# First weight sum of a Strassen piece by an adding DMA, mixer tiles that share homes, and one more k-tile pair per unit in that form

## The chip, the cores and the metric

One core of a Trainium2 chip runs the whole program. The metric is the time of one execution in device microseconds; a kernel's time is the median of its runs. Engines are named as in the profile: PE (matrix), DVE (vector), ACT (scalar), POOL (GpSimd), SP (which issues most loads).

## The reference

One layer of a decoder trunk in float32: batch 1, 256 positions (S), width 4096 (D), two token mixers of width 2048 side by side.

```
u    = rmsnorm(x) * norm_w
proj = u @ w_in                          # 4096 x 24576
a_q, a_f, a_i, a_g, b_q, b_k, b_v, b_g, gate_a, gate_b = split(proj)
o_a  = rmsnorm(hgrn2(a_q, a_f, a_i)) * silu(a_g)          # 16 heads of 128, chunks of 64
o_b  = rmsnorm(diff_attention(a pair of maps, ALiBi)) * 0.8 * silu(b_g)   # 8 heads of 2 x 128
y    = sigmoid(gate_a) * (o_a @ w_branch_a) + sigmoid(gate_b) * (o_b @ w_branch_b)
out  = rmsnorm(x + y @ w_out) * final_w
```

The four matrix products read some 537 MB of weights; everything between them is small.

## The kernel before

**Units and pieces.** The weights come as 512 *pieces*, each a pair of k-tiles (2 x 128 rows) by 1024 columns: a tile `w` of 128 x 2048 floats, one load of 1 MB. A *unit* makes 256 x 1024 outputs, in four PSUM banks of 128 x 512 (block 2t+n: row half t, column half n). There are 16 mixer units (`w_mix`; 16 pieces each), 8 gate units (`w_gate`; 16), 8 branch half units (`w_branch`; 8) and 4 output units (`w_out`; 16). `run` (L245) goes through the pieces in order.

**Three products for one.** Every float32 operand is split into hi (its value rounded to the multiplier's format) and lo (the rest), and each product is hi·hi + hi·lo + lo·hi: three matmuls (L289). Weights are split as they come: ACT writes `hi` (L165), DVE `lo` = w - hi (L166), in chunks of 1024 columns. In the mixers and in gate 0 `hi` and `lo` have five buffers each, from gate 1 on seven (L978).

**Two forms of a piece.** A plain piece (P) is two chunks and 2 x 4 blocks x 3 = 24 matmuls. A Strassen piece (S, Winograd's form with seven products in place of eight) is 7 x 3 = 21 matmuls, for which weights and activations are first added up. Its activation sums are made once per k-tile pair (`s_form`, L378, tile `sf`). Its weight sums are made for each piece (`sums`, L142, all on DVE): L146 adds two quarters of the tile in place, L147 subtracts a third from that into a tile `wt`, L151 subtracts `wt` from two quarters in place. Then four chunks are split, the third of 512 columns (`wt`), the others of 1024. PE takes the chunks in this order, and ORDER (L266) says into which banks: chunk 0 to p5 and P1 (two helper banks), chunk 1 to blocks 0 and 1, chunk 2 to P6, chunk 3 to P7 and block 2.

**Which pieces are S.** SPLIT = (4, 6, 8, 10, 12, 13) in mixer units 3 to 15 and in gates 0 and 1, SPLIT_G = (0, 2, 4, 6, 8, 10, 12, 13, 14) in gates 2 to 6, Y_SPLIT = (0, 2, 4, 6, 8, 10, 12) in output units 1 to 3: 13 x 6 + 12 + 45 + 21 = 156 pieces.

**Raw tiles and queues.** `w` has three buffers. SP issues the load of piece k as soon as the last `lo` of piece k-3 has been made (L133), so each buffer goes round: load, split, load. POOL issues the writes to DRAM (`g_dram` L374, `o_dram` L708, `h_dram` L612) and a few masks (L828, L894) in program order; a POOL instruction that waits holds up all behind it. Evictions and splits are recorded at a higher priority (L158, L293), and the order on each engine follows from that.

**End of a unit.** The last piece is held back and run block by block, (0,0), (0,1), (1,0), (1,1), six matmuls each, so that banks are emptied while PE goes on. In a unit with S pieces P6 and P7 go through DVE (L318 to L324) as soon as the last S piece is done, then the four blocks (L372 in a gate, then the sigmoid on ACT, L373, and the write, L374). Which block of the next unit PE starts with follows from the order in which the banks are emptied.

**Mixers.** Eight groups of two units: four HGRN2, four attention. Between the matmuls of a unit `step` (L224) hands out small jobs from a list. Each group's tiles come from `tmp`, one buffer for each tag; `finish` (L673) makes the norm, the gate and the transposed output.

Of the kernel before, what the change touches and what calls it, by code (L numbers as in the profile page):

```python
# [37 lines left out]
SPLIT_AHEAD = 3  # L38
# [5 lines left out]
def trunk_kernel(ctx, tc, xT, x, nw, w_mix, w_gate, w_branch, w_out, lbt, hnw, lamv, slw, fw, out):  # L44
# [8 lines left out]
    wt = ctx.enter_context(tc.tile_pool(name="wt", bufs=1))  # L53
    sp = ctx.enter_context(tc.tile_pool(name="sp", bufs=6))
# [41 lines left out]
    class Stream:  # L96
# [3 lines left out]

        def __init__(self):
# [19 lines left out]
        def load_to(self, n):  # L121
            while self.loaded < min(n, len(self.src)):
# [4 lines left out]
                if i > 1:  # L127
                    m = HALF if i < HEAD else PIECE
                    for c in range(0, PIECE, m):
                        self.load_part(i, c, m)  # L130
# [11 lines left out]
        def sums(self, i, c):  # L142
            w = self.raw[i]
            if c == 0:
                t = self.raw[i, "T"] = wt.tile([P, 512], F32, name="wt", tag="wt")
                dve.tensor_tensor(w[:, 0:512], w[:, 0:512], w[:, 512:1024], op=ALU.add)  # L146
                dve.tensor_tensor(t, w[:, 0:512], w[:, 1536:2048], op=ALU.subtract)  # L147
            if c == 2:
                t = self.raw[i, "T"]
                b = w[:, 512:1536].rearrange("p (a c) -> p a c", a=2)  # L150
                dve.tensor_tensor(b, b, t.unsqueeze(1).to_broadcast([P, 2, 512]), op=ALU.subtract)  # L151

        def split_to(self, n):
            while self.done < min(n, len(self.chunks)):
# [3 lines left out]
                with tc.high_priority(AHEAD):  # L158
                    if self.kind[i] == "S":
                        self.sums(i, c)  # L160
                    t = self.raw[i, "T"] if c == 2 else self.raw[i][:, (0, 1024, 0, 512)[c] :]
# [5 lines left out]
                if c == (3 if self.kind[i] == "S" else 1):  # L167
                    del self.raw[i]
                    self.raw.pop((i, "T"), None)
# [96 lines left out]
    ORDER = (("p5", "P1"), (0, 1), ("P6",), ("P7", 2))  # L266
# [174 lines left out]
    SPLIT = (4, 6, 8, 10, 12, 13)  # L441
    SPLIT_G = (0, 2, 4, 6, 8, 10, 12, 13, 14)
    us = {}
    s_pools = [sp] * 6
# [19 lines left out]
    def more_sums(n):  # L464
        if n == 0:
            s_pools[:] = [sp2] * 3
# [50 lines left out]
    def branch_unit(q):  # L517
# [28 lines left out]
        def post(n):  # L546
            if n == 0:
                g_load(0)
                if q == 0:
                    o_end()  # L550
                    s_pools[:] = [sp] * 6 + [sp2]
# [106 lines left out]
    with tc.tile_pool(name="tmp", bufs=1) as tmp:  # L658
# [8 lines left out]
        def half(tag):  # L667
            return tmp.tile([P, HPG, P], F32, name=tag, tag=tag)

# [3 lines left out]
        def finish(T, seg, eps, scale, slot):  # L673

            n = 1024 // seg
            o, sq, g = T["o"], T["sq"], T["g"]

            def stats():
                ss = tmp.tile([P, n], F32, name="ss", tag="ss", bufs=2)
                dve.tensor_reduce(ss, fl(sq).rearrange("p (n c) -> p n c", c=seg), axis=AX.X, op=ALU.add)  # L680
                act.activation(ss, ss, AF.Sqrt, scale=1.0 / seg, bias=eps)
                dve.reciprocal(ss, ss)
                T["ss"] = ss

            def gate():
                sg = big("z")
# [344 lines left out]
```

## Time and profile before

| | |
|---|---|
| median of 3 runs | 2794.47 us (2794.36 to 2796.64) |
| the profiled execution's own time | 2795.3 us |
| its span in the trace | 2793.6 us |
| PE, DVE, ACT, POOL busy | 99%, 79%, 57%, 3% |
| granted PE clock | 0.999 |
| bytes moved | 597.76 MB, mean 214 GB/s |

The span leaves 1.7 us of the execution's time outside. Matmuls overlap in the trace, so PE's rate is read from the time of a long row of them, and its waits from gaps that the trace lists. In the stretch from 278.5 to 1587.6 us the mixer units with S pieces and gates 0 and 1 run; gates 2 to 6 from 1587.6 to 2003 us; the branches from 2091 to 2445 us; the output units to the end.

### The profile page before, as it was taken

To read this page: it belongs to the slowest core of one execution; us is meant where nothing else is said; L and a number is where in the kernel's file an instruction comes from. 1 tells how busy PE (TensorE), PEld (TensorE's weight loads), DVE (VectorE), ACT (ScalarE), POOL (GpSimd) and SP (SyncE) were. 2 spreads that over 40 slices of the span, in tenths; PEclk is the share of its full clock that TensorE was granted. 3 is DMA by queue.
4 is the path that set the end of the run, shared out by engine and by line. 5 is a ranking of instruction groups with operands and counts; after the bars stand their busy time and mean duration, and the time that the engine had idled before them with its cause. 6 is when DMAs were issued, how large, how long until landed. Compare 5 with 4: busy or idle time off the path is not lost.

```text
span 2793.6 us, 32659 instructions
## 1 busy us (share of the span) xinstructions
PE 2770.9 (99%) x12418; PEld 2285.5 (82%) x12418; DVE 2219.3 (79%) x2502; ACT 1578.5 (57%) x1877; POOL 75.0 (3%) x124
## 2 busy tenths in 40 slices
PE   9999999999999999999999999999999999999998
PEld 7888888888888888888888888778888888888886
DVE  6784888888888888888888999999855555668997
ACT  7664656556556555565556555555553444445554
POOL 0010000000000000000000000000000000010000
PEclk9999999999999999999999999999999999999999
DMA  9555555554555555555456555555676666665665
GB/s 351 190 179 192 181 195 189 211 203 181 196 189 208 198 177 203 194 198 201 181 192 239 224 199 208 226 219 203 253 260 220 230 223 234 240 244 212 249 250 217
DMA packets 96767, 597.76 MB, mean 214 GB/s; under 512 B 11857, under 2 KB 12129, under 8 KB 31201
## 3 DMA queue, kind: packets, MB, share of 16 engines
q1 hardware_dynamic: 88272, 566.29, 56.3%
q0 software_dynamic: 8336, 29.38, 2.8%
q8 instruction: 97, 1.59, 0.2%
q14 instruction: 62, 0.50, 0.1%
HBM read 571.51 MB, written 24.12 MB: 213 GB/s over the span
## 4 chain that ended last, share of the span: by engine, by line
PE 84%; DVE 10%; DMA 3%; issue 1%; ACT 1%; POOL 0%; DVEq 0%; ACTq 0%; POOLq 0%
PE ps_w L289 82%; DVE lo L166 7%; DMA w<-in_w_gate 2%; DVE w L151 1%; ACT hi L165 1%; DMA w<-in_w_out 1%; DVE w L146 1%; PE ps_q L742 1%; DVE wt L147 0%; PE ps_sc L825 0%; PE ps_s L906 0%; DVE ut L372 0%; PE ps_o L840 0%; PE ps_y L541 0%; PE ps_t L701 0%
## 5 line engine op out<-in xcount | busy, mean ns | idle before, releaser
L165 ACT ACTIVATE hi<-w 128x1024 fp32r<-128x1024 f32 (+1 forms) x1184 | 1215.1, 1053 | 1073.9 <-PE ps_w L289 598.4
L166 DVE TENSOR_TENSOR lo<-w,hi 128x1024 fp32r<-128x1024 f32 (+1 forms) x1184 | 1415.4, 1219 | 437.1 <-ACT hi L165 423.8
L289 PE MATMUL ps_w<-hi,u 128*128 128x512 f32 x4794 | 1538.4, 391 | 1.7 <-ACT hi L165 1.6
L289 PEld LDWEIGHTS ps_w<-hi,u 128*128 128x128 f32 x4794 | 900.1, 188 | 190.3 <-ACT hi L165 3.0
L289 PE MATMUL ps_w<-lo,u 128*128 128x512 f32 x2397 | 935.0, 390 | 0.9 <-DVE lo L166 0.9
L289 PEld LDWEIGHTS ps_w<-lo,u 128*128 128x128 f32 x2397 | 450.2, 188 | 98.2 <-DVE lo L166 6.5
L289 PE MATMUL ps_w<-hi,sf 128*128 128x512 f32 x1248 | 437.0, 390 | 0.7 <-ACT hi L165 0.7
L289 PE MATMUL ps_w<-hi,oh 128*128 128x512 f32 x1024 | 317.1, 390 | 0.0
L289 PEld LDWEIGHTS ps_w<-hi,sf 128*128 128x128 f32 x1248 | 234.3, 188 | 50.1 <-ACT hi L165 1.4
L289 PE MATMUL ps_w<-hi,y 128*128 128x512 f32 x814 | 258.1, 389 | 0.0
L289 PE MATMUL ps_w<-lo,sf 128*128 128x512 f32 x624 | 244.3, 392 | 4.9 <-DVE lo L166 4.6
L289 PEld LDWEIGHTS ps_w<-hi,oh 128*128 128x128 f32 x1024 | 192.3, 188 | 39.6
L289 PE MATMUL ps_w<-lo,oh 128*128 128x512 f32 x512 | 199.2, 389 | 0.0
L151 DVE TENSOR_TENSOR w<-w,wt 128x1024 f32<-128x1024 f32 x156 | 190.4, 1220 | 0.3
L289 PEld LDWEIGHTS ps_w<-hi,y 128*128 128x128 f32 x814 | 152.8, 188 | 31.6
L289 PE MATMUL ps_w<-lo,y 128*128 128x512 f32 x407 | 158.4, 389 | 0.0
L289 PEld LDWEIGHTS ps_w<-lo,sf 128*128 128x128 f32 x624 | 117.1, 188 | 34.4 <-DVE lo L166 10.5
L146 DVE TENSOR_TENSOR w<-w 128x512 f32<-128x512 f32 x156 | 107.4, 690 | 46.5 <-DMA w<-in_w_mix 33.3
L165 ACT ACTIVATE hi<-wt 128x512 fp32r<-128x512 f32 x156 | 97.9, 627 | 36.9 <-PE ps_w L289 23.0
L289 PEld LDWEIGHTS ps_w<-lo,oh 128*128 128x128 f32 x512 | 96.2, 188 | 19.8
L147 DVE TENSOR_TENSOR wt<-w 128x512 f32<-128x512 f32 x156 | 107.5, 689 | 2.6
L166 DVE TENSOR_TENSOR lo<-wt,hi 128x512 fp32r<-128x512 f32 x156 | 107.1, 686 | 0.0
(206 smaller groups left out, 1040.6 us busy)
## 6 DMA issues: line engine op xcount, KB each, us to landing
w<-in_w_mix SPq DMA_DIRECT2D x252, 1024.0 KB, 4.8
w<-in_w_gate SPq DMA_DIRECT2D x128, 1024.0 KB, 4.9
w<-in_w_branch SPq DMA_DIRECT2D x64, 1024.0 KB, 4.9
w<-in_w_out SPq DMA_DIRECT2D x64, 1024.0 KB, 4.9
gl<-g_dram SPq DMA_DIRECT2D x32, 256.0 KB, 2.7
g_dram<-ut POOLq DMA_DIRECT2D x28, 256.0 KB, 5.3
o_dram<-s POOLq DMA_DIRECT2D x8, 512.0 KB, 6.0
ol<-o_dram SPq DMA_DIRECT2D x16, 256.0 KB, 5.4
```

Source lines behind the costliest of these rows:

```text
L146: dve.tensor_tensor(w[:, 0:512], w[:, 0:512], w[:, 512:1024], op=ALU.add)
L147: dve.tensor_tensor(t, w[:, 0:512], w[:, 1536:2048], op=ALU.subtract)
L151: dve.tensor_tensor(b, b, t.unsqueeze(1).to_broadcast([P, 2, 512]), op=ALU.subtract)
L165: act.activation(hi[:, k : k + m], t[:, k : k + m], AF.Copy)
L166: dve.tensor_tensor(lo[:, k : k + m], t[:, k : k + m], f32(hi[:, k : k + m]), op=ALU.subtract)
L289: pe.matmul(ps[b], a, w, start=first, stop=left[b] == 0)
L742: pe.transpose(ps[:, j], r[:, j * P : (j + 1) * P], ident)
```

## The change

`sums` loses its addition. The load of an S piece becomes two loads on SP (512 and 1536 columns), and POOL issues a third DMA that adds 512 columns of the weights from DRAM into the first quarter of the tile (`accum_op`); it waits for the first of the two loads. L147's difference is written in place, so the tile `wt` goes. The chunks of an S piece change places: the one that needs no sum comes first (columns 1024 to 2047, blocks 0 and 1), then the one with the DMA's sum (p5, P1); both DVE sums stand in front of the third.

SPLIT gets a seventh piece, SPLIT_G a tenth, and SPLIT_G's first two move from 0 and 2 to 1 and 3. SPLIT_AHEAD (by how many chunks splits are recorded ahead) goes from 3 to 4; `sf` has 7 + 3 buffers. In the mixers `sc`, `ee`, `kx`, `qx` and the squares lose their own tiles and use z, q, s1 and s2 again; squares and row sums come from ACT instructions with an accumulator output (one for each head and half), and `apply` takes one DVE instruction for each of these in place of two over the whole tile. That makes 13 x 7 + 14 + 50 + 21 = 176 S pieces, 20 more than before.

```diff
-SPLIT_AHEAD = 3
+SPLIT_AHEAD = 4
...
-                if i > 1:
+                if self.kind[i] == "S":
+                    self.load_part(i, 0, 512)
+                    self.load_part(i, 512, PIECE - 512)
+                    pool.dma_start(t[:, 0:512], self.src[i][:, 512:1024], accum_op=ALU.add)
+                elif i > 1:
...
-        def sums(self, i, c):
+        def sums(self, i):
             w = self.raw[i]
-            if c == 0:
-                t = self.raw[i, "T"] = wt.tile([P, 512], F32, name="wt", tag="wt")
-                dve.tensor_tensor(w[:, 0:512], w[:, 0:512], w[:, 512:1024], op=ALU.add)
-                dve.tensor_tensor(t, w[:, 0:512], w[:, 1536:2048], op=ALU.subtract)
-            if c == 2:
...
+            t2 = w[:, 1536:2048]
+            dve.tensor_tensor(t2, w[:, 0:512], t2, op=ALU.subtract)
+            b = w[:, 512:1536].rearrange("p (a c) -> p a c", a=2)
+            dve.tensor_tensor(b, b, t2.unsqueeze(1).to_broadcast([P, 2, 512]), op=ALU.subtract)
...
-                        self.sums(i, c)
-                    t = self.raw[i, "T"] if c == 2 else self.raw[i][:, (0, 1024, 0, 512)[c] :]
+                        if c == 2:
+                            self.sums(i)
+                        o = (1024, 0, 1536, 512)[c]
+                    t = self.raw[i][:, o:]
...
-    ORDER = (("p5", "P1"), (0, 1), ("P6",), ("P7", 2))
+    ORDER = ((0, 1), ("p5", "P1"), ("P6",), ("P7", 2))
...
-    SPLIT = (4, 6, 8, 10, 12, 13)
-    SPLIT_G = (0, 2, 4, 6, 8, 10, 12, 13, 14)
+    SPLIT = (4, 6, 7, 9, 10, 12, 13)
+    SPLIT_G = (1, 3, 4, 6, 7, 9, 10, 12, 13, 14)
...
             def apply():
-                o3 = fl(o).rearrange("p (n c) -> p n c", c=seg)
-                dve.tensor_tensor(o3, o3, T["ss"].unsqueeze(2).to_broadcast([P, n, seg]), op=ALU.mult)
-                dve.tensor_tensor(fl(o), fl(o), fl(T["silu"]), op=ALU.mult)
+                for i in range(n):
+                    c = slice(i * seg, (i + 1) * seg)
+                    dve.scalar_tensor_tensor(fl(o)[:, c], fl(o)[:, c], ss[:, i : i + 1], fl(T["silu"])[:, c],
+                                             op0=ALU.mult, op1=ALU.mult)
...
-                    act.activation(rows(T["o"])[:, tb], pf, AF.Copy)
-                    act.activation(rows(T["sq"])[:, tb], pf, AF.Square)
+                    o = rows(T["o"])[:, tb]
+                    for h in range(HPG):
+                        i = tb * HPG + h
+                        act.activation(o[:, h * P : (h + 1) * P], ps[:, h], AF.Square, accum_out=T["ss"][:, i : i + 1])
+                    act.activation(o, pf, AF.Copy)
```

**POOL at the end of a gate unit.** Before, POOL has nothing here but the four writes of each unit's gate tiles.

```order
L374 DMA g_dram_0_146<-ut 128x512
L374 DMA g_dram_0_148<-ut 128x512
L374 DMA g_dram_1_147<-ut 128x512
L374 DMA g_dram_1_149<-ut 128x512
L374 DMA g_dram_0_150<-ut 128x512
L374 DMA g_dram_0_152<-ut 128x512
```

Now, at the end of gate 2 (its last S pieces and gate 3's piece 1 are the first row, gate 3's piece 3 is the third):

```order
L130 DMA w<-in_w_gate 128x512 x9
L376 DMA g_dram_0_143<-ut 128x512
L130 DMA w<-in_w_gate 128x512
L376 DMA g_dram_0_145<-ut 128x512
L376 DMA g_dram_1_144<-ut 128x512
L376 DMA g_dram_1_146<-ut 128x512
L130 DMA w<-in_w_gate 128x512 x9
```

The adding DMAs stand ahead of the writes, but for that of the next unit's piece 3, which stands behind the first write.

**DVE in the middle of a gate unit.** Before, one S piece (`w_14222`) with the last `lo` of the S piece before it and the plain piece between:

```order
L146 TENSOR_TENSOR w_14222<-w_14222 128x512
L147 TENSOR_TENSOR wt_14246<-w_14222 128x512
L166 TENSOR_TENSOR lo_14207<-w_14145,hi_14206 128x1024
L166 TENSOR_TENSOR lo_14225<-w_14187,hi_14224 128x1024
L166 TENSOR_TENSOR lo_14235<-w_14187,hi_14234 128x1024
L166 TENSOR_TENSOR lo_14245<-w_14222,hi_14244 128x1024
L166 TENSOR_TENSOR lo_14255<-w_14222,hi_14254 128x1024
L166 TENSOR_TENSOR lo_14267<-wt_14246,hi_14266 128x512
L151 TENSOR_TENSOR w_14222<-w_14222,wt_14246 128x1024
L166 TENSOR_TENSOR lo_14284<-w_14222,hi_14283 128x1024
```

Now, an S piece (`w_14388`) and the plain one after it:

```order
L169 TENSOR_TENSOR lo_14413<-w_14388,hi_14412 128x1024
L169 TENSOR_TENSOR lo_14420<-w_14388,hi_14419 128x1024
L149 TENSOR_TENSOR w_14388<-w_14388 128x512
L151 TENSOR_TENSOR w_14388<-w_14388 128x1024
L169 TENSOR_TENSOR lo_14434<-w_14388,hi_14433 128x512
L169 TENSOR_TENSOR lo_14452<-w_14388,hi_14451 128x1024
L169 TENSOR_TENSOR lo_14470<-w_14429,hi_14469 128x1024
L169 TENSOR_TENSOR lo_14480<-w_14429,hi_14479 128x1024
```

One row of 512 is gone; the last `lo` of the piece follows more closely on the subtraction that it needs, by way of ACT.

**DVE and PE at the end of a gate unit.** DVE before, at the end of gate 4 (`ps_w` is a bank that is emptied; `w_14462` is the next unit's piece 0, an S piece): the four blocks in a row at the end.

```order
L320 TENSOR_TENSOR ut_14507<-ps_w_13947,ut_14498 128x512
L151 TENSOR_TENSOR w_14462<-w_14462,wt_14490 128x1024
L322 TENSOR_TENSOR ut_14498<-ut_14471,ut_14498 128x512
L166 TENSOR_TENSOR lo_14517<-wt_14490,hi_14516 128x512
L324 TENSOR_TENSOR ut_14471<-ut_14471,ut_14507 128x512
L166 TENSOR_TENSOR lo_14522<-w_14462,hi_14521 128x1024
L372 TENSOR_TENSOR ut_14476<-ps_w_13924,ut_14476 128x512
L372 TENSOR_TENSOR ut_14498<-ps_w_13928,ut_14498 128x512
L372 TENSOR_TENSOR ut_14507<-ps_w_13951,ut_14507 128x512
L372 TENSOR_TENSOR ut_14471<-ps_w_13965,ut_14471 128x512
```

DVE now (`w_14671` is the next unit's piece 0, plain; `w_14720` its piece 1, S):

```order
L169 TENSOR_TENSOR lo_14707<-w_14671,hi_14706 128x1024
L322 TENSOR_TENSOR ut_14713<-ps_w_14182,ut_14704 128x512
L374 TENSOR_TENSOR ut_14695<-ps_w_14120,ut_14695 128x512
L324 TENSOR_TENSOR ut_14704<-ut_14690,ut_14704 128x512
L169 TENSOR_TENSOR lo_14725<-w_14720,hi_14724 128x1024
L326 TENSOR_TENSOR ut_14690<-ut_14690,ut_14713 128x512
L169 TENSOR_TENSOR lo_14729<-w_14720,hi_14728 128x1024
L374 TENSOR_TENSOR ut_14704<-ps_w_14112,ut_14704 128x512
L374 TENSOR_TENSOR ut_14713<-ps_w_14124,ut_14713 128x512
L374 TENSOR_TENSOR ut_14690<-ps_w_14116,ut_14690 128x512
```

Block 0 is emptied ahead of the rest; blocks 1, 2 and 3 stand behind both first chunks of the next unit's piece 1.

PE before, in the same place: the held piece's last matmul, then piece 0's first chunk into the two helper banks.

```order
L289 MATMUL ps_w_13965<-hi_14478,u_120 128x512
L289 MATMUL ps_w_14567<-hi_14488,sf_11979 128x512
L289 MATMUL ps_w_14567<-lo_14489,sf_11979 128x512
L289 MATMUL ps_w_14567<-hi_14488,sf_11979 128x512
L289 MATMUL ps_w_14571<-hi_14488,u_113 128x512
L289 MATMUL ps_w_14571<-lo_14489,u_113 128x512
L289 MATMUL ps_w_14571<-hi_14488,u_113 128x512
L289 MATMUL ps_w_14594<-hi_14516,sf_11979 128x512
```

PE now, from the fifth of the nine matmuls of block 0 (`ps_w_14784`) with which the next unit begins, six of piece 0 and three of piece 1 (`hi_14724`):

```order
L291 MATMUL ps_w_14784<-lo_14707,u_110 128x512
L291 MATMUL ps_w_14784<-hi_14706,u_110 128x512
L291 MATMUL ps_w_14784<-hi_14724,u_110 128x512
L291 MATMUL ps_w_14784<-lo_14725,u_110 128x512
L291 MATMUL ps_w_14784<-hi_14724,u_110 128x512
L291 MATMUL ps_w_14826<-hi_14728,sf_12186 128x512
L291 MATMUL ps_w_14826<-lo_14729,sf_12186 128x512
L291 MATMUL ps_w_14826<-hi_14728,sf_12186 128x512
L291 MATMUL ps_w_14776<-hi_14697,u_110 128x512
L291 MATMUL ps_w_14776<-lo_14698,u_110 128x512
```

Behind block 0 comes p5 of piece 1 (`ps_w_14826`; its chunk holds the adding DMA's sum), then block 1 (`ps_w_14776`).

72 lines of the change are left out of this document (34 added, 38 removed).

## The prediction

> **What bounds the kernel now.** I read the page's first and fourth parts, then the list of waits, then a table by stage, then the groups.
>
> ```profile
> span 2793.6 us, 32659 instructions
> PE 2770.9 (99%) x12418; PEld 2285.5 (82%) x12418; DVE 2219.3 (79%) x2502; ACT 1578.5 (57%) x1877; POOL 75.0 (3%) x124
> PEclk9999999999999999999999999999999999999999
> PE ps_w L289 82%; DVE lo L166 7%; DMA w<-in_w_gate 2%; DVE w L151 1%; ACT hi L165 1%; DMA w<-in_w_out 1%; DVE w L146 1%; PE ps_q L742 1%; DVE wt L147 0%; PE ps_sc L825 0%; PE ps_s L906 0%; DVE ut L372 0%; PE ps_o L840 0%; PE ps_y L541 0%; PE ps_t L701 0%
> 2279.71 81.64 PE ps_w L289 x360
> PE ps_w L289 <- DVE lo L166: 5.5, 10, 0.9
> PE ps_w L289 <- ACT hi L165: 2.3, 4, 1.2
> ```
>
> PE is busy in every slice at the full granted clock, and the chain is L289 for 82%. The fifth row, from the chain in order of time, gives the rate: 81.64 / 360 = 0.2268 us for a matmul of 512 columns. The last two say that PE hardly ever waits. So a matmul fewer is 0.2268 us less, as long as what feeds PE keeps up. Where that is close, the table by stage tells: gates 2 to 6 and, below them, mixer unit 3. Its columns are stretch, length, busy PE, PEld, DVE, ACT and POOL, clock, DMA share and GB/s.
>
> ```profile
> 1587.63:1668.55 80.92, 80.92 (x359) 67.01 (x357) 75.85 (x85) 47.90 (x56) 1.61 (x3) 1.00 0.60 219
> 1668.55:1751.85 83.30, 82.34 (x358) 66.63 (x357) 78.61 (x85) 48.32 (x56) 2.16 (x4) 1.00 0.57 214
> 1751.85:1835.12 83.27, 82.11 (x359) 66.64 (x357) 77.92 (x85) 50.40 (x58) 2.16 (x4) 1.00 0.56 214
> 1835.12:1920.15 85.03, 82.46 (x358) 66.54 (x357) 80.36 (x88) 47.84 (x55) 2.16 (x4) 1.00 0.57 212
> 1920.15:2003.01 82.86, 82.15 (x358) 66.63 (x357) 77.87 (x84) 51.00 (x57) 2.16 (x4) 1.00 0.58 215
> 278.54:366.26 87.72, 87.72 (x409) 73.03 (x408) 75.43 (x81) 58.35 (x71) 2.53 (x2) 1.00 0.54 192
> ```
>
> A gate unit of 9 S pieces has 357 matmuls, 357 x 0.2268 = 81.0 us; the last four of the five gates (rows 2 to 5) take 82.9 to 85.0, with DVE busy for about 94%. There DVE is the bound, by 2 to 4 us a unit. Here are two of the waits, each a matmul whose `lo` came late, one near the start of gate 4 and one 3 us into gate 7, the only gate before whose piece 0 is plain:
>
> ```profile
> 1755.05 0.50 PE L289 MATMUL ps_w<-lo,sf 128*128 128x512 f32 x1 [0.75 <-DVE lo L166]
> 2006.08 0.50 PE L289 MATMUL ps_w<-lo,u 128*128 128x512 f32 x1 [0.64 <-DVE lo L166]
> ```
>
> **The change: matmuls.** 20 more pairs in S form are 60 matmuls fewer: 3 in each of 15 units (mixers 3 to 15, gates 0 and 1), 3 in each of gates 2 to 6. In the 15, PE is fed without a break (mixer unit 3 above, and the whole mixer stage below has one wait of 0.8 us), so they get 45 x 0.2268 = **10.2 us** shorter.
>
> ```profile
> PE ps_at L928 <- DVE ee L919: 0.8, 1, 0.8
> L166 DVE TENSOR_TENSOR lo<-w,hi 128x1024 fp32r<-128x1024 f32 (+1 forms) x1184 | 1415.4, 1219 | 437.1 <-ACT hi L165 423.8
> L165 ACT ACTIVATE hi<-w 128x1024 fp32r<-128x1024 f32 (+1 forms) x1184 | 1215.1, 1053 | 1073.9 <-PE ps_w L289 598.4
> L146 DVE TENSOR_TENSOR w<-w 128x512 f32<-128x512 f32 x156 | 107.4, 690 | 46.5 <-DMA w<-in_w_mix 33.3
> L147 DVE TENSOR_TENSOR wt<-w 128x512 f32<-128x512 f32 x156 | 107.5, 689 | 2.6
> L151 DVE TENSOR_TENSOR w<-w,wt 128x1024 f32<-128x1024 f32 x156 | 190.4, 1220 | 0.3
> 1740.95 0.69 DVE L166 TENSOR_TENSOR lo<-wt,hi 128x512 fp32r<-128x512 f32 x1
> 1741.55 1.22 DVE L151 TENSOR_TENSOR w<-w,wt 128x1024 f32<-128x1024 f32 x1
> 1742.69 3.50 DVE L166 TENSOR_TENSOR lo<-w,hi 128x1024 fp32r<-128x1024 f32 x3
> ```
>
> **DVE.** By the last three rows, instructions in a row start 0.60 us (512 columns) and 1.14 us (1024) apart, though each lasts 0.69 and 1.22. An S piece then costs DVE 4 x 1.14 + 3 x 0.60 = 6.36 us before (three 1024-column splits and L151; L146, L147 and the short split) and 5.76 after; a P piece 2.28; the eight evictions of a unit 4.8. A gate unit: 9 x 6.36 + 7 x 2.28 + 4.8 = 78.0 before (the last four gates have 77.9 to 80.4), 10 x 5.76 + 6 x 2.28 + 4.8 = 76.1 after, against 354 x 0.2268 = 80.3 us on PE. So in the middle of gates 2 to 6 PE becomes the bound, narrowly.
>
> **The end of a gate unit.** Here the change adds a wait. Piece 0 of gates 3 to 6 was S and began in helper banks; now it is plain, as in gate 7 already, and wants the unit's own banks, which PE takes as DVE empties them: after the held piece come nine matmuls of block 0 (pieces 0 and 1), then three of p5, whose chunk `lo_14729` holds an adding DMA's sum, then block 1. From the start of the held piece, 24 x 0.2268 = 5.44 us long: block 0 is complete after six matmuls, 1.36 + 0.16 us (a matmul lasts 0.39 in the next row, 0.23 of it within the 1.36), so its L374 ends near 2.2. Behind it on DVE are L324, a split, L326, a split, and block 1's L374: starts 0.60, 1.14, 0.60, 1.14 apart, so that it starts at 1.52 + 0.60 + 0.60 + 1.14 + 0.60 + 1.14 = 5.6 and ends at 6.3, wanted at 5.44 + 12 x 0.2268 = 8.2. The split of p5's chunk ends near 5.7, wanted at 5.44 + 9 x 0.2268 = 7.5. With DVE ahead nothing is lost. If DVE is only just in time (two splits, some 2.3 us, still before all this), that split ends near 8.0 and block 1 near 8.6: 0.5 and at most 0.4 lost, near the 0.64 of gate 7.
>
> So gates 2 to 6 take 80.3 us each and what waits are left: at least 0; at most what they have now, (80.92 + 83.30 + 83.27 + 85.03 + 82.86 - 5 x 81.0) / 5 = 10.4 / 5 = 2.1. I take the middle, 1.0, as DVE's work is now 4 us below PE's, but the ends can still cost their 0.6 to 0.9. 5 x 81.3 = 406.5 against 415.4: **8.9 us** gained (3.4 to 13.9).
>
> ```profile
> L289 PE MATMUL ps_w<-hi,u 128*128 128x512 f32 x4794 | 1538.4, 391 | 1.7 <-ACT hi L165 1.6
> w<-in_w_gate SPq DMA_DIRECT2D x128, 1024.0 KB, 4.9
> gl<-g_dram SPq DMA_DIRECT2D x32, 256.0 KB, 2.7
> y_dram<-yt POOLq DMA_DIRECT2D x16, 256.0 KB, 6.2
> yl<-y_dram POOLq DMA_DIRECT2D x16, 256.0 KB, 5.1
> fwt<-in_fw POOLq DMA_DIRECT2D x8, 256.0 KB, 5.7
> SPq L133 <- DVE lo L166: 2288.0, 489, 11.5
> q1 hardware_dynamic: 88272, 566.29, 56.3%
> 1756.56 2.33 POOL L374 DMA_DIRECT2D g_dram<-ut  x4 [81.37 <-ACT ut L373]
> ```
>
> **The adding DMA.** No trace row shows one. Call A the time from the issue of an S piece's first load to the sum in place. Loads wait for a free buffer (L133's 2288 us), so A counts in the round of a buffer: A, then split (1.05 on ACT, 1.22 on DVE), L147's 0.69, L151's 1.22, the last split (1.05, 1.22): A + 6.45 us. PE gives three pieces S, S, P 66 x 0.2268 = 14.97 us, so up to **A = 8.5** nothing is lost. Bounds: both parts as fast as a 256 KB load of SP, 2.7 + 2.7 = 5.4; the first part landing only with its whole piece and the second like POOL's slowest kind, 4.9 + 6.2 = 11.1. I take 2.7 + 5.1 = **7.8**, since `yl` has the same queue, direction and size and, like this, a load of 1 MB beside it. So it costs nothing: what hides it is the lead of the splits over PE. A late A first uses up that lead. Piece 4's last chunk takes a buffer that PE gives back 12 matmuls before the piece, is split 2.27 us later and is needed 15 matmuls into it: 2.7 - 2.3 + 3.4 = 3.8 us. A mixer unit has three S-to-S links on one buffer (4, 7, 10, 13), a gate four (1 to 13), so the loss is 3 x (A - 8.5) - 3.8 in each of 15 units and 4 x (A - 8.5) - 3.8 in each of 5.
>
> The adding DMA reads two sources. The Trainium skill, Collectives: The Full Stack, section on the bandwidth ceiling, says that a DMA that adds runs at about half the rate of a copy, for its two reads and not for the addition. At q1's rate above (566.29 MB in 56.3% of 2793.6 us, 360 MB a ms) the second read of 256 KB would be an estimated 0.7 us more, A = 8.5, and the sum the same; no run here shows it.
>
> POOL, in program order, now waits at each adding DMA for a first load. Behind it stand the gate writes, read again only in the branches, and masks, which go with matmuls a unit later or with PE's spare steps. Four issues took 2.33 us there, so 176 more cost POOL some 0.58 x 176 = 102 us of a queue 3% busy. 176 x 256 KB are 46 MB, 46/566 of 56.3%: 5 points of DMA share. Both lie beside PE's work; at A above 8.5 that cover is gone.
>
> **Mixer tiles.** DVE loses a reduction and two products in each of eight groups and gets 32 and 16 short instructions; ACT trades 16 squares for 48.
>
> ```profile
> L680 DVE TENSOR_REDUCE ss<-s 128x8 f32<-128x1024 f32 (+1 forms) x8 | 9.7, 1218 | 4.5 <-ACT s L946 2.9 <-ACT s L845 1.6
> L693 DVE TENSOR_TENSOR s<-s,ss 128x1024 f32<-128x1024 f32 x8 | 9.8, 1222 | 0.1
> L919 DVE SCALAR_TENSOR_TENSOR ee<-ee,sm 128x128 f32<-128x128 f32 (+1 forms) x16 | 6.6, 413 | 0.1
> L915 ACT ACTIVATE ee<-ee,nm 128x128 f32<-128x128 f32 (+1 forms) x32 | 14.3, 447 | 4.4 <-DVE nm L913 4.3
> L915 ACT ACTIVATION_READ_ACCUMULATOR ee<-ee,nm 128x1 f32 x32 | 6.0, 188 | 0.0
> ```
>
> DVE: -9.7 - 2 x 9.8 + 48 x 0.41 = -9.6 us. ACT: 48 x (0.45 + 0.19) = 31 us, less the 16 squares: at most 1.9 in each of 16 units, where it is busy 58 of 88 us. PE's work hides both; without that, a group's six squares would hold up splits by some 3.8 us at most, the lead itself. The shared homes order steps that already follow one another (norm before turn, turn before the next group's first tile). Nothing for these, nor for SPLIT_AHEAD: the buffers stay five.
>
> **Sum.** 10.2 + 8.9 = 19.1 us. Against the profiled execution (2795.3 us, span 2793.6 and 1.7 outside) 2776.2; the median shown is 0.8 lower, so **2775.5 us**, -0.7%. With the waits in the gates at their ends it is 2770.5 to 2781.
>
> **Rivals.**
> 1. *DVE stays the bound in gates 2 to 6; about no change.* L149, L151, ACT's `hi` and the last split now follow closely, with one split of 512 columns and no other piece's work between, and each S piece stands behind a sum that comes by DMA. If that leaves DVE idle 0.5 us in six of the ten S pieces, it is 3.0 us a unit; and the gates' own idle time now, 83.30 - 78.0 = 5.3, may stay as it is. Then a unit takes 76.1 + 5.3 + 3.0 = 84.4, five 422, 6.6 more than now, and the time is 2794.5 - 10.2 + 6.6 = 2791. For it: DVE is busy for only 94% where it is the bound, so the 5.3 are waits that its order makes. Against: its load falls by 1.9 us in a unit, and the splits are recorded one chunk further ahead.
> 2. *The sum comes too late; slower.* POOL's DMA shares its 16 engines with the rest of its own piece and comes in behind it: the 1 MB load's 4.9, then `fwt`'s 5.7, A = 10.6. Then 15 x (3 x 2.1 - 3.8) + 5 x (4 x 2.1 - 3.8) = 60.5 us are lost, 2836. It decides from 65 x (A - 8.5) - 76 = 19.1, A = 9.96. At the upper bound, 11.1, it is 93 us, 2868. This rival also holds the case that *the change doesn't do what it says*: an adding DMA that waits for both loads of its piece is later by the second load, which is this price. For it: 5.1 to 6.2 for 256 KB on POOL's queue against 2.7 on SP's. Against: `yl` lands in 5.1 among loads of 1 MB, and the first quarter is loaded first.
>
> By the page named above rival 2 would have A = 11.3 and an estimated 2881 us.
>
> **How the numbers follow.** Forecast 0.66. Rival 2 0.16: of the bounds 5.4 to 11.1, 1.1 of 5.7 lie above 9.96, less a little since `yl` is nearest 7.8. Rival 1 0.18. A difference of 0.2% (5.6 us) is about what can be told from no change here. Rival 1 lies within it for the most part, with a little on either side: faster 0.66 + 0.05 = 0.71, same 0.13, slower 0.16. The range leaves out most of rival 2: 2769 (2770.5 less what lies between two executions, 2796.64 - 2794.36 = 2.3 at most) to 2802 (rival 1, or rival 2 at its start, 2775.5 + 65 x 1.58 - 76 = 2802 at A = 10.08).
>
> **What would show it.** Right: 60 matmuls fewer at 0.227 us; the 15 units 0.7 us shorter each; gates 2 to 6 at about 81 us, with under 1 us of PE's waits, most of them at the ends; sums in place within 8.5 us of the first load's issue. Wrong: rows of waits of `hi` on an adding DMA with PE behind them, growing from piece 7 to piece 13 (rival 2); gates above 83 us with waits of `lo` spread over them (rival 1); or a rate of matmuls other than 0.2268.

## The result, and the profile after

The changed kernel takes 2979.05 us (median of 4 runs, 2970.76 to 2983.49) against 2794.92 before (also of 4): a ratio of 1.0651 (95% interval 1.0638 to 1.0664), 184 us more where 19 less were forecast. It is the second rival, beyond its upper bound of 2868. The profiled execution took 2979.9 us. First the page's head, and the groups of one line that PE and POOL carry (busy time, mean ns of one, idle time before it and what ended it):

```profile
span 2978.2 us, 33626 instructions
PE 2834.6 (95%) x12358; PEld 2277.2 (76%) x12358; DVE 2190.8 (74%) x2456; ACT 1610.6 (54%) x1998; POOL 231.6 (8%) x300
L291 PE MATMUL ps_w<-lo,sf 128*128 128x512 f32 x704 | 293.9, 418 | 83.5 <-DVE lo L169 81.0
L291 PE MATMUL ps_w<-hi,sf 128*128 128x512 f32 x1408 | 508.9, 400 | 18.8 <-ACT hi L168 18.5
L130 POOL DMA_DIRECT2D w<-in_w_mix x91 | 77.0, 846 | 865.7 <-DMA w<-in_w_mix 530.5
```

The 60 matmuls are gone (12418 to 12358), but PE is busy for 95% where it was 99%, and most of its idle time (102 of 144 us) stands ahead of matmuls with `sf`, which only S pieces have. Idle time has grown by 121 us of the 184. The rest is inside PE's busy time, which is 64 us longer for fewer matmuls: a matmul in a row takes up 0.23 us, but counts as busy for 0.39 or more where the next one is late, and some ran at half the clock (last section). The table by stage, in the same columns as before: mixer unit 3, gates 2 to 6, output unit 2.

```profile
285.28:376.52 91.24, 88.62 (x406) 72.00 (x405) 75.58 (x79) 59.33 (x73) 9.02 (x9) 1.00 0.64 205
1668.09:1756.85 88.76, 84.46 (x354) 66.93 (x355) 74.14 (x80) 49.55 (x56) 9.31 (x12) 0.98 0.67 210
1756.85:1856.39 99.54, 87.13 (x356) 67.50 (x354) 78.78 (x81) 51.38 (x58) 10.81 (x14) 0.97 0.67 210
1856.39:1957.88 101.49, 87.92 (x355) 66.82 (x354) 77.65 (x81) 51.41 (x58) 10.73 (x14) 0.97 0.65 199
1957.88:2057.33 99.45, 88.35 (x355) 68.63 (x354) 77.79 (x80) 49.97 (x57) 10.76 (x14) 0.95 0.66 207
2057.33:2163.62 106.29, 90.51 (x355) 67.61 (x354) 78.67 (x81) 53.27 (x61) 9.92 (x13) 0.95 0.63 195
2778.68:2874.53 95.85, 84.95 (x364) 67.58 (x364) 72.18 (x77) 46.63 (x56) 9.29 (x13) 0.99 0.71 222
```

DVE's work in a gate is about what was forecast (74 to 79 us for 76.1), yet the gates take 89 to 106: neither PE nor DVE is the bound any more. What is, the chain in order of time says, which the profile follows back to 1984 us; here are pieces of it in gates 5 and 6 and in output unit 2 (start, length, what):

```profile
1993.07 6.50 DMA w<-in_w_gate
2008.77 4.23 DMA w<-in_w_gate
2013.02 0.04 POOLq L130
2013.55 6.27 DMA w<-in_w_gate
2031.23 6.27 DMA w<-in_w_gate
2056.39 7.99 DMA w<-in_w_gate
2803.86 9.69 DMA w<-in_w_out x2
```

The second to fourth rows are a first load, POOL's queue behind it, and the adding DMA; the first, fifth and sixth are adding DMAs too, and the four follow one another by 18 to 25 us. In all, twelve pieces of transfers, 64 us, stand on the chain in these two gates; before has three there, 17 us, all in gate 5. The DMA issues (KB each, median us from issue to landing):

```profile
w<-in_w_mix SPq DMA_DIRECT2D x93, 256.0 KB, 3.5
w<-in_w_mix POOLq DMA_DIRECT2D x91, 256.0 KB, 5.6
w<-in_w_gate SPq DMA_DIRECT2D x64, 256.0 KB, 3.7
w<-in_w_gate POOLq DMA_DIRECT2D x64, 256.0 KB, 6.3
w<-in_w_out SPq DMA_DIRECT2D x21, 256.0 KB, 5.7
w<-in_w_out POOLq DMA_DIRECT2D x21, 256.0 KB, 4.7
```

Paired piece by piece (A is, as in the forecast, the time from the issue of an S piece's first load to the sum in place), the first part lands 3.5 us after its issue (median of the 91 pieces in mixers), POOL's DMA is issued at 4.1 and the sum is in place at **A = 10.0 us**; in gates 2 to 6 it is 11.0, in output units 10.7. One round of a raw buffer in mixer unit 5 (piece 7, then piece 10, in the same buffer): the two issues of SP, and DVE and ACT between them.

```profile
491.73 0.80 SPq L137 DMA_DIRECT2D w<-in_w_mix  x2
495.93 0.84 POOL L130 DMA_DIRECT2D w<-in_w_mix  x1 [10.28 <-DMA w<-in_w_mix]
502.44 1.06 ACT L168 ACTIVATE hi<-w 128x1024 fp32r<-128x1024 f32 x1 [0.30 <-PE ps_w L291]
503.44 0.69 DVE L149 TENSOR_TENSOR w<-w 128x512 f32<-128x512 f32 x1
505.78 1.22 DVE L151 TENSOR_TENSOR w<-w 128x1024 f32<-128x1024 f32 x1
507.12 4.86 ACT L168 ACTIVATE hi<-w 128x1024 fp32r<-128x1024 f32 x5 [2.24 <-PE ps_w L291]
508.21 3.50 DVE L169 TENSOR_TENSOR lo<-w,hi 128x1024 fp32r<-128x1024 f32 x3 [1.21 <-ACT hi L168]
509.47 0.81 SPq L137 DMA_DIRECT2D w<-in_w_mix  x2
```

The sum is in place at 501.71, A = 9.98. Then come `hi` (502.44), L149, L151 (505.78, behind the split of what it overwrites), the last `hi` (507.12) and the last `lo` (508.21), and the buffer goes out again at 509.47: 7.76 us after the sum. The round is 17.74 us, for three pieces S, P, S that PE does in 66 x 0.2268 = 14.97.

### The profile page after: what moved, and what is told of

The parts are those of the page before. It is cut to its first block, busy times and chain, and to the rows that moved or that the text cites. A ratio compares the mean times of both kernels' runs of the same rounds, so it can differ in the third digit from the quotient of the medians.

```text
span 2978.2 us, 33626 instructions
## 1 busy us (share of the span) xinstructions
PE 2834.6 (95%) x12358; PEld 2277.2 (76%) x12358; DVE 2190.8 (74%) x2456; ACT 1610.6 (54%) x1998; POOL 231.6 (8%) x300
## 5 line engine op out<-in xcount | busy, mean ns | idle before, releaser
L169 DVE TENSOR_TENSOR lo<-w,hi 128x1024 fp32r<-128x1024 f32 (+1 forms) x1380 | 1550.8, 1152 | 683.4 <-ACT hi L168 679.2
L168 ACT ACTIVATE hi<-w 128x1024 fp32r<-128x1024 f32 (+1 forms) x1380 | 1333.8, 997 | 1254.7 <-PE ps_w L291 556.0
L291 PE MATMUL ps_w<-hi,u 128*128 128x512 f32 x4594 | 1493.0, 393 | 15.0 <-DVE ut L374 13.9
L291 PE MATMUL ps_w<-lo,u 128*128 128x512 f32 x2297 | 901.1, 392 | 1.0 <-DVE lo L169 1.0
L291 PE MATMUL ps_w<-hi,sf 128*128 128x512 f32 x1408 | 508.9, 400 | 18.8 <-ACT hi L168 18.5
L291 PE MATMUL ps_w<-lo,sf 128*128 128x512 f32 x704 | 293.9, 418 | 83.5 <-DVE lo L169 81.0
L291 PE MATMUL ps_w<-hi,y 128*128 128x512 f32 x814 | 260.1, 391 | 7.0 <-DVE ut L609 7.0
L151 DVE TENSOR_TENSOR w<-w 128x1024 f32<-128x1024 f32 x176 | 215.4, 1224 | 4.6
L130 POOL DMA_DIRECT2D w<-in_w_mix x91 | 77.0, 846 | 865.7 <-DMA w<-in_w_mix 530.5
L149 DVE TENSOR_TENSOR w<-w 128x512 f32<-128x512 f32 x176 | 120.8, 687 | 8.9 <-DMA w<-in_w_out 7.9
L130 POOL DMA_DIRECT2D w<-in_w_gate x64 | 54.4, 850 | 553.1 <-DMA w<-in_w_gate 237.4
L291 PEld LDWEIGHTS ps_w<-lo,y 128*128 128x128 f32 x407 | 76.9, 189 | 16.0
```

Source lines behind the costliest of these rows:

```text
L130: pool.dma_start(t[:, 0:512], self.src[i][:, 512:1024], accum_op=ALU.add)
L149: dve.tensor_tensor(t2, w[:, 0:512], t2, op=ALU.subtract)
L151: dve.tensor_tensor(b, b, t2.unsqueeze(1).to_broadcast([P, 2, 512]), op=ALU.subtract)
L168: act.activation(hi[:, k : k + m], t[:, k : k + m], AF.Copy)
L169: dve.tensor_tensor(lo[:, k : k + m], t[:, k : k + m], f32(hi[:, k : k + m]), op=ALU.subtract)
L291: pe.matmul(ps[b], a, w, start=first, stop=left[b] == 0)
```

## The experiments

Lengths of stages in the profiled executions, from the start of a unit's first matmul to that of the next unit's, in us:

| kernel | ratio to before (95%) | mixers 1, 2 | mixers 3-15, gate 0 | gate 1 | gates 2-6 | outputs 1-3 |
|---|---|---|---|---|---|---|
| before | 1 | 182.8 | 1225.9 | 83.2 | 415.4 | 260.1 |
| changed | 1.0651 (1.0638-1.0664) | 189.4 | 1284.6 | 98.3 | 495.5 | 284.6 |
| e1 DVE sums | 1.0157 (1.0142-1.0172) | 189.5 | 1238.3 | 84.0 | 435.3 | 259.6 |
| e4 no first load | 1.0012 (1.0003-1.0022) | 188.4 | 1228.2 | 83.5 | 411.5 | 259.1 |
| e7 copy for add | 1.0404 (1.0388-1.0419) | 189.6 | 1258.2 | 94.8 | 470.4 | 271.3 |
| e2 old pieces | 1.0308 (1.0287-1.0328) | 182.8 | 1240.6 | 92.9 | 455.4 | 282.1 |
| e3 four raw | 1.0020 (1.0011-1.0029) | 182.8 | 1227.6 | 83.1 | 415.8 | 261.6 |
| e13 no first, old pieces | 0.9972 (0.9959-0.9984) | 182.8 | 1228.1 | 83.1 | 408.7 | 259.2 |

Stages that wait vary from one execution to the next: e6 below, whose edit is in the gates, has 278.0 us in output units where the changed kernel has 284.6.

**Is it the sum, and its lateness?** e1 gives the sum back to DVE, e4 has the quarter in place early, e7 copies where the change adds. Their edits to the S piece's loads:

```diff
 e1
-                if self.kind[i] == "S":
...
-                elif i > 1:
+                if i > 1:
...
+                        if c == 1:
+                            w = self.raw[i]
+                            dve.tensor_tensor(w[:, 0:512], w[:, 0:512], w[:, 512:1024], op=ALU.add)
 e4
-                    self.load_part(i, 0, 512)
+                    pool.dma_start(t[:, 0:512], self.src[i][:, 512:1024])
                     self.load_part(i, 512, PIECE - 512)
-                    pool.dma_start(t[:, 0:512], self.src[i][:, 512:1024], accum_op=ALU.add)
 e7
-                    pool.dma_start(t[:, 0:512], self.src[i][:, 512:1024], accum_op=ALU.add)
+                    pool.dma_start(t[:, 0:512], self.src[i][:, 512:1024])
```

> The changed kernel, but each S piece comes in one load of 1 MB again and DVE makes its first sum (one more instruction of 512 columns, 0.60 us); pieces, order of the chunks and shared tiles as changed. Theory (the sum comes too late: 10.0 us from the first load's issue to the sum in place, which makes the round of a raw buffer 17.5 us where PE needs 15.0): the waits of PE on hi and lo in mixers 3 to 15, gates 0 and 1 and the output units go, those units take 0.7 us less than before the change; what is left is the 6.7 us of mixer units 1 and 2 and gates 2 to 6, where DVE has 82.1 us of work in a unit, so 83 to 87 each: 2792 to 2812 us. Rival (the new order of chunks, with L149, L151 and the splits in close succession, or the extra pieces themselves, make PE wait): mixer units stay 3 to 5 us longer, above 2880 us.

Measured: 2839.84 us, above the theory's range and far below the rival's. The mixers' waits on a DMA are gone and output units are as before; gates take 85.6 to 89.0 us, a little over the expected 83 to 87, and mixers did not gain their 0.7 but lost 0.9 each. So the adding DMA costs 139 us against a sum on DVE; the rest of the change is dearer than the theory had it.

> The changed kernel without the first of the two loads on SP: POOL loads the second quarter of the weights straight into the first (a plain DMA, 256 KB, which waits only for the buffer), so the sum is left out and the rest of the work stays. Theory (lateness of the sum): the quarter is there some 5.5 us after the buffer comes free, the waits go and gates 2 to 6 come to 81 to 83 us; with the 6.7 us of mixer units 1 and 2, 2778 to 2800 us. Rival (order of the splits on DVE and ACT): as the changed kernel, above 2940 us.

Measured: 2799.64 us, at the theory's upper end. With the quarter in place 5.4 us (median) after the first issue, 179 of the 184 us are gone, though chunks and pieces are those of the changed kernel, and DVE's order too but for 26 of 2456 instructions. The rival falls: the loss is not in the order of the splits. By itself e4 can't tell lateness from the load that it leaves out (597.8 MB moved for 644.0, and no wait for a load in POOL's queue); e7 and e3, which keep that load, can.

> The changed kernel with POOL's DMA copying instead of adding (the sum is left out), at the same place and behind the same wait for the first load. Theory: the adding itself costs little, what is late is the order (first load 3.5 us, 0.6 us until POOL goes on, 0.85 us of issue, 4.8 us until it lands): the time stays within 20 us of the changed kernel's 2979. Rival (the second read of an adding DMA takes 0.7 us of the 10.0): each of 65 links is 0.7 us shorter, 45 us less, 2934 us.

Measured: 2908.27 us, 71 less than the changed kernel: my theory was wrong on this point, and the rival nearer, though it had 45. PE, DVE, ACT and POOL have the same instructions in the same order as in the changed kernel, and the bytes moved are the same, so this is the cleanest test of lateness. The copy is issued in 0.54 us for 0.85 and lands sooner:

```profile
L130 POOL DMA_DIRECT2D w<-in_w_mix x91 | 49.1, 540 | 873.5 <-DMA w<-in_w_mix 417.8
w<-in_w_mix POOLq DMA_DIRECT2D x91, 256.0 KB, 4.6
```

4.6 us against 5.6 from issue to landing (medians), and A is 8.9 in mixers against 10.0. 71 us for 1.1 us is 65 for each us of A. That this is the forecast's factor is in part luck: A fell by 1.3 us in gates 2 to 6, and some 13 of the 71 us are in output units, which the factor leaves out. The Trainium skill, Collectives: The Full Stack, section on the bandwidth ceiling, has the adding transfers of a reduce-scatter at half the rate of copies, for their second read; the forecast's estimate of 0.7 us for that second read agrees with what is left here when the 0.31 us of issue are taken off the 1.0.

**Why does lateness cost?** e2 has the old pieces, e3 beside them a fourth raw buffer, e8 the same with DVE's sums.

```diff
 e2
+    SPLIT = (4, 6, 8, 10, 12, 13)
+    SPLIT_G = (0, 2, 4, 6, 8, 10, 12, 13, 14)
 e3 = e2, six buffers of hi, lo and sf as said below, and
...
+    wraw = ctx.enter_context(tc.tile_pool(name="wraw", bufs=4))
+LOAD_AHEAD = 4
 e8 = e3 with the loads and sums of e1
```

> The changed kernel with the S pieces of before (6 of 16 in mixers, 9 in gates), the sum still by the adding DMA. In a mixer unit only piece 10 is followed by an S piece on the same buffer (13), in a gate 10 (13) and 13 (piece 0 of the next). Theory (what counts is two S pieces in a row on one buffer, each round 2.5 us too long): the mixers lose under 1 us each, gates 2 to 6 under 4 each; 2795 to 2825 us. Rival (adding DMAs slow the kernel wherever they are, by what they take of POOL's queue and the DMA engines): the loss goes with the number of S pieces, 156/176 of 184 us, 2955 us.

Measured: 2882.88 us, between theory and rival, so both fall as they were put. In mixers A is 8.1 us (median), and most units are within 0.9 us of before. Three stages lose 3 to 4.6 us, mixer 7, mixer 12 and gate 0, and each of them has one sum that comes far later, that of piece 12: A is 13.9, 14.0 and 15.0 there. Gates 2 to 6 (A 11.2) lose 8.0 each, and output units (A 10.3) 7.3 each, though in output units S and P alternate and no S piece follows an S piece on one buffer. What matters is not the pair but how late each sum is: in these gates 11.2 and 7.8 from the sum to the next load make some 19 us, where PE's three pieces give 15.0 to 15.6. I take it that the plain piece before it cannot run ahead by the difference because its splits fill the few `hi` and `lo` buffers; no run changes their number alone.

> As e2_old_pieces (adding DMA, S pieces of before), but four raw buffers in place of three, loads recorded one piece further ahead, and, to make room, six buffers of hi and lo from gate 1 on in place of seven and the six sf buffers of before. Theory (a late sum costs because the round of a raw buffer, 10 us and 7.7 of splits, is longer than PE's three pieces, 15 to 15.6 us): PE's four pieces take 20.4 us or more, so the waits of e2 go in mixers, gates and output units, and the gates come to 81 to 83 us, since DVE has only 72.6 us of work there: 2785 to 2802 us. Rival (loads that run together on the DMA engines, or the few hi and lo buffers, make the sums late whatever the raw buffers): above 2840 us.

Measured: 2802.12 us, 81 less than e2 and a hair above the range, and this is the run that settles the mechanism for the pieces of before. Its sums are as late as ever or later:

```profile
w<-in_w_mix POOLq DMA_DIRECT2D x78, 256.0 KB, 6.2
w<-in_w_gate POOLq DMA_DIRECT2D x57, 256.0 KB, 6.3
PE 2775.0 (99%) x12418; PEld 2287.9 (82%) x12418; DVE 2123.8 (76%) x2370; ACT 1590.5 (57%) x1957; POOL 208.5 (7%) x280
```

A is 10.5 us in mixers and 10.8 in gates 2 to 6 (median; e2: 8.1 and 11.2), and yet PE is busy for 99%: with one more piece of PE's work in a buffer's round, sums as late cost next to nothing. But the gates take 415.8 us, not 5 x 81.0 = 405: DVE's free time did not become PE's.

> As e3_four_raw, but with one load of 1 MB and the first sum on DVE. It tells what the fourth buffer is worth without an adding DMA. Theory: before has no wait that a raw buffer would cure outside of gates 3 to 6, and there DVE has 78.0 us of work in either; 2788 to 2800 us. Against e3_four_raw it tells what an adding DMA is worth once its lateness is covered: 0.60 us of DVE in each of 9 pieces, in five gates, at most 10 us.

Measured: 2808.20 us (ratio 1.0043, 1.0028 to 1.0058): over the range. A fourth buffer brings DVE's own sums nothing. The adding DMA, its lateness covered, is worth about 6 us against them.

**POOL's queue.** e6 takes the gate writes out of it.

```diff
 e6
-            pool.dma_start(g_dram[2 * q + n][t], g)
+            nc.scalar.dma_start(g_dram[2 * q + n][t], g)
```

> The changed kernel with the gate tiles' writes to DRAM issued by ACT in place of POOL, so that no adding DMA stands behind one (piece 3 of gates 3 to 6 did: its adding DMA was issued 11.5 us after its first load at gate 4's start). Theory: piece 1, not piece 3, is what PE waits for at the start of a gate, so within 15 us of the changed kernel's 2979. Rival (the order of POOL's queue costs the 6 to 8 us at the start of gates 3 to 6): 2950 us or less.

Measured: 2976.07 us (ratio 1.0645, 1.0629 to 1.0661). As the theory had it, the gate writes in POOL's queue cost nothing that can be told.

**The rest of the change.** e5 has the old pieces and DVE's sums; e10 the old order of the chunks too; e11 also the tile `wt` for the difference, so that only shared tiles, squares and SPLIT_AHEAD are left (its `sf` buffers are before's as well); e9 is e3 in the old order; e12 is e3 with `wt`.

```diff
 e10 (and e9)
+    ORDER = (("p5", "P1"), (0, 1), ("P6",), ("P7", 2))
...
+                        o = (0, 1024, 1536, 512)[c]
 e12
+            if c == 1:
+                t = self.raw[i, "T"] = wt.tile([P, 512], F32, name="wt", tag="wt")
+                dve.tensor_tensor(t, w[:, 0:512], w[:, 1536:2048], op=ALU.subtract)
...
```

> The changed kernel with the first sum on DVE and the S pieces of before: what is left of the change are the shared tiles, the squares on ACT, the order of the chunks, the difference in place and splits recorded one chunk further ahead. Theory: none of these costs more than 5 us: 2790 to 2802 us; mixer unit 1 stays at 92 us as in e2. Rival (shared tiles or the order of the chunks cost some of the 184 us): above 2805 us.

Measured: 2805.84 us (ratio 1.0035, 1.0022 to 1.0047), on the rival's side by a little: some 10 us, nearly all in gates 2 to 6 (425.7 us); which part it is, the next two tell.

> As e5_sum_and_pieces_back with the order of the chunks of before too; what is left of the change are the shared tiles, the squares on ACT, the difference in place and splits one chunk further ahead. Theory (e5's 9 us come from the order of the chunks, in gates 3 to 6): 2793 to 2800 us. Rival (shared tiles or splits further ahead cost them): 2803 to 2809 us.

Measured: 2820.87 us (ratio 1.0088, 1.0074 to 1.0102). Theory and rival fall: the old order is slower by 15 us, in gates (432.9) and output units (265.4).

> The kernel before with the shared mixer tiles, the squares on ACT and splits recorded one chunk further ahead, and nothing else of the change: S pieces, their four DVE sums, the tile wt and the order of the chunks are those of before. It differs from e10_sum_pieces_order_back only in wt (there the difference is written in place over the fourth quarter). Theory (in e10 the difference in place costs the 24 us, in gates 2 to 6 and output unit 3: L149 must wait until the chunk that it overwrites has been split, where L147 could run two chunks earlier): 2793 to 2800 us. Rival (shared tiles or splits further ahead cost them, though the mixers of e10 are as long as before): 2810 us or more.

Measured: 2798.39 us (ratio 1.0006, 0.9997 to 1.0015). As expected: shared tiles, squares on ACT and SPLIT_AHEAD cost nothing that can be told; the difference in place, which has to wait for the split of what it overwrites, costs 22 us in the old order of chunks (e10). In the new order it costs 15 less (e5 beside e10), so these two parts of the change belong together.

> As e3_four_raw, but the chunks of an S piece in the order of before (the chunk with the adding DMA's sum first, into p5 and P1, then columns 1024 to 2047 into blocks 0 and 1). Theory (the new order costs PE waits at the ends of gates, since an S piece at a unit's start then wants blocks that are still to be emptied, and with four raw buffers a late sum does no harm first in line either): gates 3 to 7 lose their waits at the start, some 6 to 10 us less than e3's 2802, so 2790 to 2797 us, and no slower than before. Rival (the sum, needed first, is late again): above 2805 us.

Measured: 2811.05 us (ratio 1.0050, 1.0038 to 1.0063), 9 us slower than e3; the rival's side.

> As e3_four_raw (adding DMA, S pieces of before, four raw buffers, new order of chunks), but the difference goes into a tile wt of its own, recorded ahead of the second chunk's split. Theory (with the sum's lateness covered by the fourth buffer and the difference free of the split before it, DVE has 72.6 us of work in a gate unit and PE 81.0): gates 2 to 6 come to 81 to 82 us each, 2786 to 2797 us, as fast as before or faster. Rival (what is left in e3's gates are the starts of units, where a unit's banks are emptied, and not the difference): 2800 to 2805 us.

Measured: 3023.15 us (ratio 1.0814, 1.0799 to 1.0829): theory and rival fall. It is the slowest of all, and takes 221 us more than e3, for one instruction moved and given a tile. DVE's group of this difference in e12, then the one in place of e3:

```profile
L151 DVE TENSOR_TENSOR wt<-w 128x512 f32<-128x512 f32 x156 | 107.8, 691 | 457.6 <-DMA w<-in_w_mix 184.0
```
```profile
L149 DVE TENSOR_TENSOR w<-w 128x512 f32<-128x512 f32 x156 | 107.3, 688 | 2.0
```

The same 0.69 us of work, but 457.6 us of idle time in front of it against 2.0: recorded early, it comes to the head of DVE's queue and waits there for a sum that is in place 10.9 us after its load, and the splits of earlier pieces wait behind it. DVE's order shows it: in 116 of the 156 pieces at least three splits of earlier pieces stand behind the difference, and 446 of the 458 us of idle time are in front of these 116. In e3 the difference never stands ahead of an earlier piece's split.

**What are the extra pieces worth?** e13 is e4 with the old pieces; e14 is e11 with the new ones (and six `hi` and `lo` buffers from gate 1 on, so that only mixers and gate 0 are read).

> As e4_no_first (one plain DMA of POOL in place of load and sum, so that the sum is left out), with the S pieces of before. Theory (the extra pieces bring nothing in the mixers, since a unit with pieces 6 and 7 and 9 and 10 in a row waits 0.7 us more and has 0.7 us less to do, and cost 6.7 us in mixer units 1 and 2): the mixers are as long as in e4, and the time is 2790 to 2800 us. Rival (each extra piece brings its 0.68 us and something else of the change takes it back): 2805 to 2812 us.

Measured: 2789.96 us (ratio 0.9972, 0.9959 to 0.9984), as the theory had it: mixers 3 to 15 and gate 0 take 1228.1 us with 6 S pieces and 1228.2 with 7 (e4). The extra piece's 0.68 us is given back in waits.

> The kernel of e11_shared_tiles (before's S form with DVE's four sums and wt, before's order of chunks) with the S pieces of the change; to make room for their activation sums, six buffers of hi and lo from gate 1 on in place of seven, so only mixers and gate 0 are read. Theory (the place of the extra piece, not the adding DMA, eats its gain): mixers 3 to 15 and gate 0 within 0.4 us of before each, mixer units 1 and 2 6.7 us longer; DVE-bound gates (82.1 us of work) longer: 2805 to 2830 us. Rival (before's S form lets the extra pieces gain): those 14 units 0.5 us or more shorter each.

Measured: 2826.08 us (ratio 1.0095, 1.0081 to 1.0109). The 14 units take 1224.7 us against e11's 1224.0, within the 0.4 each on the mean (single units from -3.5 to +3.4), and mixers 1 and 2 take 7.1 longer. The pieces alone bring nothing there.

No kernel here that makes the sum is faster than before; e11 and e3 come nearest. (e13, the one that is, leaves the sum out.) No run has a fourth buffer together with the new pieces.

## Why the prediction was wrong

The kernel took 204 us more than the 2775.5 that were forecast. e4 splits this: 179 us go with the sum in place early (2979.05 - 2799.64), which the forecast had at nothing, and 24 us remain even then (2799.64 - 2775.5): the 19 of gain, and 5 of loss. Steps 1 to 4 are about the first part, 5 to 7 about the second.

1. **"I take 2.7 + 5.1 = 7.8"** is the step that failed first. A is 10.0 in mixers, 11.0 in gates 2 to 6. In mixers the first load took 3.5 us for 2.7; the 0.6 us from its landing to POOL's issue were no term of the sum; and the adding DMA took 5.6 us from its issue to its landing for 5.1 (its issue alone is 0.31 us longer than that of the copy in e7). The bound 11.1 held the median, not the single pieces: 42 of 176 are above it, up to 16.7 us in gates and 19.2 in output units. In fourteen of the sixteen above 13 us another piece's load was still under way when the first part was issued.
2. **"up to A = 8.5 nothing is lost"** was the second. The rest of the round is 7.76 us in the round shown, not 6.45: ACT waits for a `hi` buffer that PE frees, and L151 waits for the split of what it overwrites. (The median is 7.8 in gates 2 to 6 and 8.6 in mixers, with what is waited for PE in it.) That leaves 7.2. With 10.0 and 7.2 the forecast's own formula gives 3 x 2.8 - 3.8 = 4.6 us for a mixer unit; against e4, which differs in lateness and in the load that it leaves out, it is (1284.6 - 1228.2) / 14 = 4.0 in mixers 3 to 15 and gate 0. For e7 (A = 8.9) it gives 1.3, and 2.1 were lost. So the form comes near, and both sizes were off, in the same direction; but the 7.2 is read from the changed kernel itself. Gate 1, the fifteenth unit, lost 14.8 (98.3 - 83.5), which the formula does not give; half of it is in step 4.
3. **"4 x (A - 8.5) - 3.8 in each of 5"**: gates lost 16.8 us each against e4, (495.5 - 411.5) / 5, where 4 x (11.0 - 7.2) - 3.8 = 11.4. The chain does not end with the unit: piece 14's buffer goes to the next unit's piece 1, an S piece, so there are five links, and if no lead is won back between units, they make 5 x 3.8 = 19 (for e7, with A = 9.7, 12.5; lost were 11.8). Output units (25.5 us against e4) stood at nothing in the sum; e2 shows that S pieces one by one lose there too.
4. **"With DVE ahead nothing is lost"**, and 0.5 and at most 0.4 otherwise, at the end of a gate unit. The longest waits of PE at the starts of gates 2 to 6 are 7.31, 5.53, 4.59, 3.39 and 4.80 us; in e4 the first two are 1.00 and 0.75. At the first two it is the eviction L374 that PE waits for. Here are ACT, DVE (two rows) and PE at the start of gate 2:

```profile
1662.69 1.06 ACT L168 ACTIVATE hi<-w 128x1024 fp32r<-128x1024 f32 x1 [4.03 <-DMA w<-in_w_gate]
1663.78 1.23 DVE L169 TENSOR_TENSOR lo<-w,hi 128x1024 fp32r<-128x1024 f32 x1 [3.85 <-ACT hi L168]
1665.52 0.69 DVE L374 TENSOR_TENSOR ut<-ps_w,ut 128x512 f32<-128x512 f32 x1
1668.09 0.77 PE L291 MATMUL ps_w<-hi,u 128*128 128x512 f32 x1 [7.31 <-DVE ut L374]
```

   PE had begun its last matmul of gate 1 at 1660.39, so the banks were complete by 1661. But in DVE's queue the split of piece 1's second chunk stood ahead of their eviction, and it waited for the adding DMA's sum (in place at 1662.59). A late sum thus costs a second time where a queue has other work behind it. Output units have two such waits as well, for L609, 7.0 us together.
5. **"they get 45 x 0.2268 = 10.2 us shorter"**: not even in e4, with the sum in time. PE's matmuls went, at the same rate, but a seventh S piece (6 and 7, 9 and 10 in a row) left its waits in their place (e13 beside e4, e14 beside e11). "PE is fed without a break" was read from a kernel in which, as I take it, the lead was still there to be spent; no run shows the lead itself.
6. **"8.9 us gained"** in the gates: in e13, with a timely sum and nine S pieces, the gates do gain 6.7 us; the tenth piece takes 2.8 of it back (e4). In these runs the forecast's direction holds only for a sum that costs DVE nothing and is early.
7. Mixers 1 and 2, counted at nothing, cost 5.6 to 7.1 us in each kernel with seven pieces and nothing in those with six. PE waits there once, for a mask of POOL:

```profile
180.55 11.28 POOL L825 TENSOR_SCALAR_AFFINE_SELECT s<-s 128x512 f32<-128x512 f32 x2 [166.43 <-DVE u L395]
```
```profile
PEld ps_o L838 <- POOL s L825: 4.8, 1, 4.8
```

Rival 2 had the mechanism (a late sum makes a buffer's round too long) and its place in mixers and gates, but not the size: its dearest case was 2868. It named a turning point, A = 9.96, and its chance of 0.16 was the share of the bounds above that point. The bounds held the median; the middle came from a sum with a term left out, and the turning point, with 7.2 for 8.5, lies at 8.7. Rival 1 (DVE's order in gates) was real as well, at some 10 us with DVE's own sums (e5), but hidden under the other.

## What to carry to other kernels

To take work off a busy engine and give it to a dependent DMA, add up the whole round of the buffer first: every issue, every hand-over between queues (0.6 us here) and every landing under load, then the work until the buffer is free; compare that with what the consumer does in the same round, and give the buffer another copy if it doesn't fit (e3). A wait that is long is harmless at the end of a queue and dear at the head of one that others share (e12, and the starts of gates 2 and 3). Where an engine is at 99% because others run a little ahead of it, work taken from it may shorten the lead too: the 60 matmuls fewer brought nothing even in e4.

## What the runs showed of the hardware

PE's granted clock falls to half behind waits of a few us, or two of under 1 us close together. In the changed kernel the trace has eleven such stretches before its end, of 3.4 or 6.8 us each, all in or right behind waits of PE. Here is the table for 3.6 us behind two waits (4.59 and 1.07 us) at the start of gate 4, and for 3.3 us behind two of 0.62 and 0.77 us that end within 2 us of each other in mixer unit 5, with the granted clock third from the right:

```profile
1865.40:1869.00 3.60, 3.60 (x9) 2.82 (x9) 3.21 (x5) 2.08 (x4) 1.68 (x3) 0.50 0.83 205
527.90:531.20 3.30, 3.30 (x10) 2.59 (x9) 3.30 (x4) 1.54 (x2) 0.26 (x1) 0.53 0.83 279
```

Matmuls start 0.427 us apart there in place of 0.227. In these stretches the changed kernel has 85 matmuls that start 0.40 to 0.45 us apart, some 17 us of the 184; before has none, e3 7, e12 256.

The mask of POOL is the other: a select of 128 x 512 that takes 0.63 us when DVE is idle took 10.70 us in mixer unit 1, where DVE was busy without a pause until 0.5 us before its end (6.42 us in before, whose DVE has one activation sum less there; 10.70 in e4 and e14 too). The Trainium skill, GPSIMD Engine Reference, section Architecture, says that POOL's SBUF ports are shared with DVE; the two durations agree with it, though no run here took DVE's work away to show it.
